# Order of work at a phase edge: spatial mixing put two steps earlier and kept in other tiles, half of a combination of h put into the next phase

## The chip, the cores and the metric

The kernel runs on one core of one Trainium2 chip. Its time is the device time of one execution in microseconds (us); several runs are given by their median and their extremes. Traces come from single profiled executions, and all stretches of time are counted from the start of such an execution's span.

## The reference

The reference computes one layer of a gated decoder with three parallel branches, for a prompt of 1024 tokens and for 8 x 8 sample tokens that share the weights (1088 tokens, width 1024). Cut to its core:

```python
h = rmsnorm(x, norm_g) * (1.0 + scale) + shift            # shift, scale, gate from silu(c) @ ada_w
z = h @ w_in + b_in                                       # one wide projection, columns split by use
vn = rmsnorm(a_v, gmlp_vnorm_g)                           # branch A: spatial gating
s = einsum('gts,bnsgc->bntgc', tril(gmlp_ws), vn) + gmlp_bs
ya = a_u * s * silu(a_g)
yb = sink_attention(...) * silu(b_g)                      # branch B: window of 128
yc = mlstm(...) * sigmoid(o) * silu(c_g)                  # branch C
gates = sigmoid(m_g)                                      # three gates per channel
merged = gates_a * (ya @ w_branch_a) + gates_b * (yb @ w_branch_b) + gates_c * (yc @ w_branch_c)
x_out = x + gate * (merged @ w_out)
```

## The kernel before

All operands are float32. A matrix is kept as two float32r parts, hi and lo (hi a rounded copy, lo what is left), and a product is three matmuls: hi·hi, hi·lo, lo·hi. So every operand must be split: a cast on ScalarE (ACT) writes hi, a subtraction on VectorE (DVE) writes lo. `hh[k]` and `hl[k]` are the two parts of h, 128 channels (k = 0 to 7) by 1088 tokens.

**Two phases meet here.** In the phase before the edge TensorE (PE) works on attention in 26 steps. In each step one pipeline stage of several blocks is issued (`q`, `s`, `p`, `v`, `y` of `Prompt` or `Sample`), and between them a filler of projection matmuls, the last of which make the gate of branch B (`bg_chunk`, tile `zb`). The order of PE's instructions is written out by hand in this phase (`manual_schedule`); in the others, and on the other engines, a scheduler orders instructions, and each engine takes its own in that order. The table `tail` gives what is added after certain steps. `Sample.v` ends in three small VectorE operations on the tile `ots`, and the transpose in `Sample.y` reads it.

**Spatial mixing.** `mix(g)` for the four channel groups is 18 matmuls (`pk<-WT,vn`, `pk<-WTs,vn`) into three PSUM banks and three VectorE evictions into the tile `sA[g]` (lines 1264 and 1269). Of the banks `pk` there are three in all, so a second mix waits for the evictions of the first. Before, the mixing of groups 0 and 1 follows steps 21 and 22, that of groups 2 and 3 follows step 25, the end of the phase.

**The last phase** forms a 2 x 2 block product in seven products instead of eight. For the weights of two column groups, and for h cut in two halves of its channels (k and k + 4) and of its tokens (b = 0, 1, each `HT` = 544), product q multiplies a combination of weights with a combination of h, `TT[q, k]`, k = 0 to 3. `TT[1]`, `TT[2]` and `TT[3]` are plain parts of h. `TT[5]` (`t_first`) and `TT[6]` (`t_second`) are made long before the edge. `TT[4]` (`t_third`: subtract twice, add, split into a tile `tc`) is made after steps 22, 23 and 25 in halves of 272. `TT[7]` (`t_in_place`) overwrites the second half of `hh[k]` and `hl[k]`, k = 0 to 3, which nothing reads afterwards in its old form; `x` and `y` in it are one tile. A product of one item is two halves of 272 tokens with 12 matmuls each, three for each k. `collect` gathers the results on VectorE.

**Weights of the last phase.** `seven(...)` makes the items of one pair of columns: a preparation (load `raw`, combine in `comb`, split into `prod` by `w_split`, lines 1365 and 1366) and a run. Preparations are issued five items ahead. There are five `raw` tiles and six `prod` tiles, so the split of a weight waits for the product six weights earlier. `items` lists the order in which products run. Group 0 of `it` runs its products in the order 1, 2, 5, 6, 3, 7, 4, the other groups in the order 1, 6, 7, 5, 3, 2, 4. Before, the list begins with all of `t_in_place`, then products 1, 2, 5, 6, 3 of group 0, product 1 of group 1, products 7 and 4 of group 0, and products 6 and 7 of group 1.

**Tiles.** `slot(tag, ...)` gives a named piece of SBUF that later tiles with this tag take over. A tile waits until the users of the one before it are done.

Of the kernel before, what the change touches and what calls it, by code (L numbers as in the profile page):

```python
# [37 lines left out]
def trunk_kernel(ctx: ExitStack, tc: tile.TileContext, I, O):  # L38
# [762 lines left out]
    drow = dp.tile([9, 1024], F32, name="drow")  # L801
    TT = {}
    sA = [None] * 4

# [14 lines left out]
    with tc.tile_pool(name="bph", bufs=1, side="right", reuse_waits="tile") as b1:  # L819
# [264 lines left out]
        class Sample:  # L1084
# [48 lines left out]
            def v(self):  # L1133
                g, bg = self.g, self.bg
                pO = pu_()
                mm(pO[:, 0:64], self.PT[:64, 128:256], vB[:64, 8, g], True, True)
                for b in range(4):
                    mm(pO[32 * b:32 * b + 32, 64:128], self.PT[:, 32 * b:32 * b + 32], vcn[0][:, 4 * bg + b, g], True, True)
                self.ot = bt([128, 64], "ots", bufs=2)
                V.tensor_copy(self.ot, pO[:, 0:64])  # L1140
                V.tensor_tensor(self.ot, self.ot, pO[:, 64:128], ALU.add)
                V.tensor_scalar(self.ot, self.ot, self.dn, 0.5, ALU.mult, ALU.mult)

# [55 lines left out]
        def t_tile(tag):  # L1199
            t = slot(tag, [128, 2, HT], F32R, name="tc")  # L1200
            return t[:, 0], t[:, 1]
# [25 lines left out]
        def t_third(k):  # L1227
            to = t_tile(("m4", "m5", "y6", "m0")[k])
            for j in range(2):
                t_next(gt(HC, "tx"), 4, k, k + 4, 0, 6, to, slice(HC * j, HC * j + HC))  # L1230
# [25 lines left out]
        def mix(g):  # L1256
            sA[g] = slot(("y2", "y3", "y7", "m1")[g], [128, NT], name="sA")
            bsb, WT = A["bsb"], A["WT"]
# [17 lines left out]
        def seq(*fs):  # L1276
            return lambda: [f() for f in fs]

        tail = {0: lambda: t_first(0), 1: lambda: t_first(1), 2: lambda: t_first(2), 3: lambda: t_first(3), 11: lambda: t_second(0), 13: lambda: t_second(1), 17: lambda: t_second(2),
                18: seq(lambda: t_second(3), a_scale), 20: a_load, 21: lambda: mix(0),  # L1280
                22: seq(lambda: mix(1), lambda: t_third(0)), 23: lambda: t_third(1),
                25: seq(lambda: mix(2), lambda: mix(3), lambda: t_third(2), lambda: t_third(3))}

# [79 lines left out]
    def w_split(x, tile=None):  # L1363
        t = tile if tile is not None else w2.tile([128, 2, 512], F32R, tag="prod", bufs=6, name="prod")
        S.copy(t[:, 0], x)  # L1365
        V.tensor_tensor(t[:, 1], x, t[:, 0].bitcast(F32), ALU.subtract)  # L1366
        return t

    def wk(t, part, k, n=128):
# [132 lines left out]
    def t_in_place(k):  # L1502
# [5 lines left out]
        TT[7, k] = t_split(x, half(hh, k, 1), half(hlo, k, 1))  # L1508

    def y_tiles(f):  # L1510
        yh[f] = y2[0].tile([128, NT], F32R, tag=f"yh{f}", name="yh")
        yl[f] = slot(("y2", "y3", "y7")[f - 1], [128, NT], F32R, name="yl") if f else y2[0].tile([128, NT], F32R, tag="yl0", name="yl")

# [38 lines left out]
    def y_load(n):  # L1552
        br = ORDER_BR[n]
        if not stage:
            stage.append(slot("m1", [128, 2, HT], name="stage"))
        for f in range(4):
# [88 lines left out]
    gr = [x for g in range(4) for x in gate_rows(g)]  # L1645
    items += [act(t_in_place, *((k,) for k in range(4)))] + it[0][:5] + it[1][:1] + it[0][5:]
    rest = it[1][1:3] + [None] + it[1][3:4] + [None] + it[1][4:5] + [None] + it[1][5:6] + [None] + it[1][6:] + [None]
    rest += it[2][:1] + [None] + it[2][1:2] + [None] + it[2][2:3] + [None] + it[2][3:] + it[3]
    items += [x or gr.pop(0) for x in rest]

    def gate_b(f, b):
        if not stage:
            stage.append(slot("m1", [128, 2, HT], name="stage"))
        x, y = stage[0][:, 0], stage[0][:, 1]
# [41 lines left out]
    KS8 = (0, 4, 1, 5, 2, 6, 3, 7)  # L1696
    SLOTS = (None, ("m4", "m5", "y6", "m0"), ("y0", "y1", "m2", "m3"), ("y4", "y5", "y2", "y3"))
    wo = {}
# [73 lines left out]
```

## Time and profile before

| what | us |
|---|---|
| median of 3 runs | 1217.87 |
| lowest, highest | 1213.67, 1218.21 |
| profiled execution, its time | 1217.25 |
| profiled execution, its span | 1215.5 |

The span is the stretch in which instructions run. A page gives the busy time of each engine, the span in 40 slices, the chain of waits and the costliest groups of instructions. In a group, `out<-in` are the program's names, L and a number is the line. PE is TensorE's matmuls, PEld its weight loads, DVE VectorE, ACT ScalarE, POOL GpSimd. A row of waits has the total, the count and the longest. A row of a table by windows has for each engine the busy time and the number of instructions that start there, then the clock that TensorE was granted (1.00 is full), the busy share of the DMA engines and GB/s.

| slices of 1/40 of the span (30.4 us) | 16 to 21 |
|---|---|
| from, to | 486 to 668 us |
| PE, tenths busy | 9 9 9 9 7 9 |
| DVE, tenths busy | 7 7 5 6 9 7 |

The edge between the two phases lies in the fifth of these.

### The profile page before, as it was taken

The page shows a single profiled execution, that of the slowest core. Times are in us where ns is not written, and L with a number is a line of the kernel's source. Part 1 is how long each engine was busy: PE and PEld are TensorE (multiplying, and loading weights), DVE is VectorE, ACT ScalarE, POOL GpSimd, SP SyncE. Part 2 cuts the span into 40 slices and gives each one's busy share as a digit, 9 for nine tenths or more (in the row PEclk, how much of TensorE's full clock was granted, in tenths as well). Part 3 has the DMA queues.
Part 4 walks back from the last instruction along what each step waited for, and adds up shares of the span by engine and source line. Part 5 has one row for each costly group of instructions (what it writes and reads, how often), then busy time and mean ns, then how long its engine had stood idle before and what let it go on. Part 6 is the DMA issues. An engine that isn't in the chain of part 4 may idle for free.

```text
span 1215.5 us, 23135 instructions
## 1 busy us (share of the span) xinstructions
PE 1166.3 (96%) x8900; PEld 1116.6 (92%) x8900; DVE 787.7 (65%) x1887; ACT 485.4 (40%) x1215; POOL 76.9 (6%) x111
## 2 busy tenths in 40 slices
PE   5899999999979999999979999999999999999998
PEld 2689999999969998888878999999999999999998
DVE  3477877755465677775697784655766676669333
ACT  3443454433432367896243432333333343236000
POOL 2100001011022110010100000000000000000000
PEclk8989999999989999999989999999999999999999
DMA  9731222233222210213233246523533354466332
GB/s 310 224 88 36 73 66 79 57 106 102 79 72 67 64 43 20 70 40 97 63 87 106 81 134 197 153 81 94 169 111 110 109 167 126 127 197 192 96 92 83
DMA packets 150773, 129.74 MB, mean 107 GB/s; under 512 B 13613, under 2 KB 140213, under 8 KB 150648
## 3 DMA queue, kind: packets, MB, share of 16 engines
q1 hardware_dynamic: 142984, 118.96, 33.4%
q0 software_dynamic: 2240, 7.08, 1.6%
q10 hardware_dynamic: 5440, 2.23, 0.7%
q8 instruction: 70, 1.15, 0.4%
q14 instruction: 39, 0.32, 0.1%
HBM read 99.39 MB, written 29.82 MB: 106 GB/s over the span
## 4 chain that ended last, share of the span: by engine, by line
PE 53%; DVE 3%; ACT 3%; DMA 1%; issue 1%; SPq 0%; ACTq 0%; DVEq 0%
PE pg L84 21%; PE pk L84 18%; PE pu L84 12%; ACT vn L1254 1%; DMA raw<-in_w_in_dram 0%; ACT Sm L1043 0%; DMA raw<-in_w_out_dram 0%; PE pu L88 0%; DVE prod L1366 0%; DVE sA L1264 0%; ACT hl L123 0%; ACT Sm L1051 0%; DVE ml L1573 0%; DVE tx L1219 0%; DVE wo L1366 0%
## 5 line engine op out<-in xcount | busy, mean ns | idle before, releaser
L84 PE MATMUL pg<-hl,hl 128*128 128x256 f32 (+3 forms) x904 | 279.1, 309 | 0.2 <-DVE hl L388 0.2
L84 PE MATMUL pg<-hh,hl 128*128 128x384 f32 (+1 forms) x912 | 240.9, 338 | 2.5 <-DVE hh L387 1.6
L84 PE MATMUL pg<-hl,hh 128*128 128x256 f32 (+1 forms) x1008 | 179.1, 285 | 0.2 <-ACT pg L1193 0.2
L84 PEld LDWEIGHTS pg<-hl,hl 128*128 128x128 f32 x904 | 172.3, 191 | 3.2 <-DVE hl L388 1.9
L84 PEld LDWEIGHTS pg<-hh,hl 128*128 128x128 f32 x912 | 163.8, 191 | 7.1 <-DVE hh L387 3.0
L84 PEld LDWEIGHTS pg<-hl,hh 128*128 128x128 f32 x1008 | 151.8, 190 | 0.7 <-ACT pg L1193 0.4
L1365 ACT CAST prod<-raw 128x512 fp32r<-128x512 f32 x76 | 47.2, 621 | 124.4 <-PE pk L84 62.0
L84 PE MATMUL pg<-hh,prod 128*128 128x272 f32 x400 | 84.7, 291 | 5.4 <-DVE prod L1366 3.0
L84 PE MATMUL pk<-hh,prod 128*128 128x272 f32 x368 | 78.6, 292 | 1.6 <-ACT hh L812 1.6
L84 PEld LDWEIGHTS pg<-hh,prod 128*128 128x128 f32 x400 | 66.7, 191 | 5.8 <-DVE prod L1366 3.2
L1366 DVE TENSOR_TENSOR prod<-raw,prod 128x512 fp32r<-128x512 f32 x76 | 52.1, 687 | 23.4 <-ACT prod L1365 23.3
L1365 ACT CAST prod<-comb 128x512 fp32r<-128x512 f32 x64 | 39.4, 616 | 65.4 <-PE pk L84 30.1
L1490 ACT ACTIVATE tt<-tt,bh 128x272 f32<-128x272 f32 x96 | 49.9, 523 | 38.9 <-DVE tt L1463 14.7
L84 PEld LDWEIGHTS pk<-hh,prod 128*128 128x128 f32 x368 | 61.7, 191 | 3.1 <-ACT hh L812 1.8
L84 PE MATMUL pk<-tc,prod 128*128 128x272 f32 x444 | 61.7, 288 | 0.0
L84 PE MATMUL pg<-yh,prod 128*128 128x272 f32 x288 | 60.1, 288 | 0.0
L84 PE MATMUL pk<-yh,prod 128*128 128x272 f32 x288 | 60.0, 288 | 0.0
L84 PEld LDWEIGHTS pk<-tc,prod 128*128 128x128 f32 x444 | 57.8, 188 | 0.9 <-DVE tt L1532 0.4
L84 PE MATMUL pg<-hl,prod 128*128 128x272 f32 x200 | 58.1, 290 | 0.0
L84 PE MATMUL pg<-tc,prod 128*128 128x272 f32 x408 | 57.5, 291 | 0.0
L84 PE MATMUL pk<-hl,prod 128*128 128x272 f32 x184 | 53.7, 292 | 1.0 <-DVE hl L813 1.0
L84 PEld LDWEIGHTS pg<-tc,prod 128*128 128x128 f32 x408 | 54.1, 191 | 0.4 <-issue 0.4
(512 smaller groups left out, 2630.0 us busy)
## 6 DMA issues: line engine op xcount, KB each, us to landing
raw<-in_w_in_dram SPq DMA_DIRECT2D x124, 256.0 KB
dmg<-tt SPq DMA_DIRECT2D x88, 136.0 KB
mprev<-dmg SPq DMA_DIRECT2D x64, 136.0 KB
adaraw<-in_ada_w_dram SPq DMA_DIRECT2D x16, 512.0 KB
stage<-dy SPq DMA_DIRECT2D x24, 272.0 KB
xt<-in_x_prompt_dram SPq DMA_DIRECT2D x8, 512.0 KB
graw<-in_ada_w_dram SPq DMA_DIRECT2D x16, 256.0 KB
raw<-in_w_out_dram SPq DMA_DIRECT2D x32, 128.0 KB
```

Source lines behind the costliest of these rows:

```text
L84: T.matmul(out, lhsT=lhsT, rhs=rhs, start=start, stop=stop)
L1254: S.activation(vn[g][:tn, n], vn[g][:tn, n], AF.Copy, scale=vq[:tn, n:n + 1])
L1365: S.copy(t[:, 0], x)
L1366: V.tensor_tensor(t[:, 1], x, t[:, 0].bitcast(F32), ALU.subtract)
L1490: S.activation(x, x, AF.Tanh, bias=bh[:, b:b + 1], scale=0.5)
```

## The change

The evictions of the mixing of groups 2 and 3 go to the tiles m4 and m5 instead of y7 and m1; those held vn of groups 0 and 1, the inputs of the mixing of groups 0 and 1. With that, group 2 is mixed after step 22 and group 3 after step 23. `t_third` of k = 0 and 1 follows steps 24 and 25 and writes y6 and m0. For k = 2 and 3 it is taken out of this phase: `t_late` makes `TT[4]` there in one piece of 544 instead of two of 272, in y7 and m1. The three operations on `ots` get a high priority with the scheduler.

In the last phase `t_in_place` no longer stands at the head of the list. It is issued in two parts, behind the split of the second and of the fourth weight; `t_late` follows behind that of the sixth. Products 7 and 4 of group 0 no longer follow one another: product 6 of group 1 comes between.

```diff
@@ tiles of TT[4]
+    T4S = ("y6", "m0", "y7", "m1")
@@ Sample.v
                 self.ot = bt([128, 64], "ots", bufs=2)
-                V.tensor_copy(self.ot, pO[:, 0:64])
-                V.tensor_tensor(self.ot, self.ot, pO[:, 64:128], ALU.add)
-                V.tensor_scalar(self.ot, self.ot, self.dn, 0.5, ALU.mult, ALU.mult)
+                with tc.high_priority():
+                    V.tensor_copy(self.ot, pO[:, 0:64])
+                    V.tensor_tensor(self.ot, self.ot, pO[:, 64:128], ALU.add)
+                    V.tensor_scalar(self.ot, self.ot, self.dn, 0.5, ALU.mult, ALU.mult)
@@ t_third, mix
-            to = t_tile(("m4", "m5", "y6", "m0")[k])
+            to = t_tile(T4S[k])
...
-            sA[g] = slot(("y2", "y3", "y7", "m1")[g], [128, NT], name="sA")
+            sA[g] = slot(("y2", "y3", "m4", "m5")[g], [128, NT], name="sA")
@@ tail
-                22: seq(lambda: mix(1), lambda: t_third(0)), 23: lambda: t_third(1),
-                25: seq(lambda: mix(2), lambda: mix(3), lambda: t_third(2), lambda: t_third(3))}
+                22: seq(lambda: mix(1), lambda: mix(2)), 23: lambda: mix(3), 24: lambda: t_third(0), 25: lambda: t_third(1)}
@@ w_split and what is issued behind a split
-        S.copy(t[:, 0], x)
-        V.tensor_tensor(t[:, 1], x, t[:, 0].bitcast(F32), ALU.subtract)
+        a = S.copy(t[:, 0], x)
+        b = V.tensor_tensor(t[:, 1], x, t[:, 0].bitcast(F32), ALU.subtract)
+        splits.append((a.ins, b.ins))
         return t
+
+    splits = []
+
+    def behind(f, n, *ks):
+        def run(_):
+            with tc.issue_after(splits[n][0]), tc.issue_after(splits[n][1]):
+                for k in ks:
+                    f(k)
+
+        return (None, run)
@@ the last phase
+    def t_late(k):
+        x = y2[0].tile([128, 2, HT], F32, tag="yh1", name="tx")[:, 0]
+        t_next(x, 4, k, k + 4, 0, 6, t_tile(T4S[k]), slice(0, HT))
...
-        yl[f] = slot(("y2", "y3", "y7")[f - 1], [128, NT], F32R, name="yl") if f else y2[0].tile([128, NT], F32R, tag="yl0", name="yl")
+        yl[f] = slot(("y2", "y3", "m4")[f - 1], [128, NT], F32R, name="yl") if f else y2[0].tile([128, NT], F32R, tag="yl0", name="yl")
...
-            stage.append(slot("m1", [128, 2, HT], name="stage"))
+            stage.append(slot("m5", [128, 2, HT], name="stage"))
...
-    items += [act(t_in_place, *((k,) for k in range(4)))] + it[0][:5] + it[1][:1] + it[0][5:]
-    rest = it[1][1:3] + [None] + it[1][3:4] + [None] + it[1][4:5] + [None] + it[1][5:6] + [None] + it[1][6:] + [None]
+    items += it[0][:2] + [behind(t_in_place, 1, 0, 1)] + it[0][2:4] + [behind(t_in_place, 3, 2, 3)] + it[0][4:5] + it[1][:1]
+    items += [behind(t_late, 5, 2, 3)] + it[0][5:6] + it[1][1:2] + it[0][6:]
+    rest = it[1][2:3] + [None] + it[1][3:4] + [None] + it[1][4:5] + [None] + it[1][5:6] + [None] + it[1][6:] + [None]
...
-    SLOTS = (None, ("m4", "m5", "y6", "m0"), ("y0", "y1", "m2", "m3"), ("y4", "y5", "y2", "y3"))
+    SLOTS = (None, ("y7", "m1", "y6", "m0"), ("y0", "y1", "m2", "m3"), ("y4", "y5", "y2", "y3"))
```

Three places in the order of the engines. TensorE, the end of the attention phase: `pk<-WT,vn` and `pk<-WTs,vn` are a mix, `pu<-ident,ots` the transpose in `Sample.y`, `pg<-hh,hl` and `pg<-hl,hl` the filler, and `pg<-hh_250,prod` the first matmul of the last phase (a number behind hh or hl tells the tiles apart).

```order
 L84 MATMUL pg<-hl_569,hl 128x320
 L84 MATMUL pg<-hh_568,hl 128x320
+L84 MATMUL pk<-WT,vn 128x128 x8
+L84 MATMUL pk<-WTs,vn 128x64
 L88 MATMUL pu<-ident,ots 64x128
 L84 MATMUL pu<-vB,PTs 128x64
 L84 MATMUL pu<-vcn,PTs 32x64 x4
 L88 MATMUL pu<-ident,ots 64x128
-L84 MATMUL pk<-WT,vn 128x128 x8
-L84 MATMUL pk<-WTs,vn 128x64
-L84 MATMUL pk<-WT,vn 128x128 x8
-L84 MATMUL pk<-WTs,vn 128x64
```

Behind the last transpose of an attention output there were two mixes; now there is none, and one of them has moved ahead of these transposes (the other lies further ahead).

VectorE, the head of the last phase. `tx` is the scratch tile of the combinations of h, `tc` the lo part of `TT[4]`, `sA` an eviction of the mixing, `prod<-raw` the lo part of a weight, `hl_251<-tx` the lo part of `TT[7]`. Before:

```order
L1264 SCALAR_TENSOR_TENSOR sA<-pk,cols,bsb 128x512
L1269 SCALAR_TENSOR_TENSOR sA<-pk,cols,bsb 128x64
L813 TENSOR_TENSOR tc<-tx,tc 128x272 x3
L1505 TENSOR_TENSOR tx<-hh_387,hh_250 128x544
L1506 TENSOR_TENSOR tx<-hl_388,hl_251 128x544
L1507 TENSOR_TENSOR tx<-tx 128x544
L1366 TENSOR_TENSOR prod<-raw_7086,prod 128x512
L813 TENSOR_TENSOR hl_251<-tx,hh_250 128x544
L1366 TENSOR_TENSOR prod<-raw_7088,prod 128x512
```

The change:

```order
L1266 SCALAR_TENSOR_TENSOR sA<-pk,cols,bsb 128x512
L1271 SCALAR_TENSOR_TENSOR sA<-pk,cols,bsb 128x64
L1219 TENSOR_TENSOR tx<-hh_387,tc 128x272 x2
L1142 COPY ots<-pu 128x64
L1220 TENSOR_TENSOR tx<-tx,tc 128x272 x2
L1143 TENSOR_TENSOR ots<-ots,pu 128x64
L1221 TENSOR_TENSOR tx<-tx,hl_388 128x272 x2
L1144 TENSOR_SCALAR ots<-ots,dns 128x64
L814 TENSOR_TENSOR tc<-tx,tc 128x272
```

The last eviction of the mixing used to stand directly ahead of the last splits of `TT[4]`; now all of `t_third` for k = 0 and 1 stands behind it. The first weight follows at the end of that block:

```order
L1221 TENSOR_TENSOR tx<-tx,hl_404 128x272 x2
L814 TENSOR_TENSOR tc<-tx,tc 128x272 x2
L1367 TENSOR_TENSOR prod<-raw_7060,prod 128x512
L1367 TENSOR_TENSOR prod<-raw_7062,prod 128x512
L1517 TENSOR_TENSOR tx<-hh_387,hh_250 128x544
L1518 TENSOR_TENSOR tx<-hl_388,hl_251 128x544
```

The first two weights are split ahead of the first in-place combination, which used to stand ahead of them.

VectorE, behind the last part of `TT[7]`, where the results of product 7 of group 0 are used (`tt`, `tg` and `yl` are results, gate and output of group 0). Before:

```order
L1544 SCALAR_TENSOR_TENSOR tt<-tg,tt 128x272
L1480 TENSOR_TENSOR tt<-pk,tt 128x272
L1543 SCALAR_TENSOR_TENSOR tt<-tt,cols 128x272
L1366 TENSOR_TENSOR prod<-raw_7145,prod 128x512
L1360 TENSOR_TENSOR comb<-raw_7629,raw_7631 128x512
L1548 TENSOR_TENSOR yl<-tt,yh 128x272
```

The change:

```order
L1220 TENSOR_TENSOR tx<-tx,tc 128x544
L1559 SCALAR_TENSOR_TENSOR tt<-tt,cols 128x272
L1367 TENSOR_TENSOR prod<-raw_7157,prod 128x512
L1221 TENSOR_TENSOR tx<-tx,hl_569 128x544
L1564 TENSOR_TENSOR yl<-tt,yh 128x272
L1361 TENSOR_TENSOR comb<-raw_7617,raw_7619 128x512
L1462 TENSOR_TENSOR tt<-pk,tt 128x272
L1560 SCALAR_TENSOR_TENSOR tt<-tg,tt 128x272
L814 TENSOR_TENSOR tc<-tx,tc 128x544
```

`t_late` for k = 3 stands between the work on the results, and its last row is what product 4 of group 0 reads.

More of the change, by code (lines that the diff above doesn't have):

```diff
@@ L1652, in gate_b @@
         if not stage:
-            stage.append(slot("m1", [128, 2, HT], name="stage"))
+            stage.append(slot("m5", [128, 2, HT], name="stage"))
         x, y = stage[0][:, 0], stage[0][:, 1]
```

## The prediction

> **What bounds the kernel now.** First the page: how much of the span TensorE works.
>
> ```profile
> span 1215.5 us, 23135 instructions
> ...
> PE 1166.3 (96%) x8900; PEld 1116.6 (92%) x8900; DVE 787.7 (65%) x1887; ACT 485.4 (40%) x1215; POOL 76.9 (6%) x111
> ```
>
> TensorE (PE) is busy 96% of the span, so a change that leaves the matmuls as they are, as this one does, can only move the gaps in between. The windows table shows where they are around the edge between the two phases.
>
> ```profile
> 600.00:612.00 12.00, 7.04 (x48) 6.26 (x47) 11.36 (x31) 4.13 (x13) 0.54 (x1) 0.86 0.08 20
> 612.00:620.00 8.00, 4.97 (x23) 4.84 (x22) 7.86 (x14) 3.09 (x6) 0.00 (x0) 0.58 0.00 0
> 620.00:640.00 20.00, 17.41 (x137) 16.99 (x136) 19.45 (x37) 8.42 (x16) 0.00 (x0) 1.00 0.47 132
> ...
> 660.00:700.00 40.00, 40.00 (x329) 36.19 (x329) 32.06 (x76) 16.35 (x35) 0.00 (x0) 1.00 0.30 88
> ...
> 800.00:900.00 100.00, 100.00 (x800) 100.00 (x799) 60.58 (x123) 34.82 (x66) 0.00 (x0) 1.00 0.40 115
> ```
>
> The columns are length, PE, PEld, DVE (VectorE), ACT, POOL, granted clock, DMA share, GB/s. From 600 to 640 PE misses 5.0 + 3.0 + 2.6 = 10.6 us, and VectorE is the engine that is full: 38.7 of 40. Later PE is full, so what is late there is late at the end, one for one. The waits of PE name the gaps:
>
> ```profile
> PE pg L84 <- DVE prod L1366: 3.0, 1, 3.0
> PE pu L88 <- DVE ots L1142: 2.5, 1, 2.5
> PE pg L84 <- ACT prod L1365: 2.4, 1, 2.4
> ...
> PE pk L84 <- ACT hh L812: 1.6, 1, 1.6
> PE pk L84 <- DVE hl L813: 1.0, 1, 1.0
> ```
>
> 5.4 us wait for the first split weight (prod), 2.5 for the last sample's attention output (ots), 2.6 for the in-place combination that product 7 reads (hh, hl). All three hang on one queue. VectorE alone, in two windows:
>
> ```profile
> 589.90:604.60 14.70, 11.16 (x35) 0.95 0.21 63
> 604.70:639.40 34.70, 34.47 (x67) 0.88 0.27 76
> ```
>
> From 604.7 until the last hl is split VectorE works 34.47 of 34.70 us. So the question is not which wait is removed, but **where the work of VectorE goes, and which product of TensorE stands behind it**.
>
> **The change, part by part.** Durations on VectorE:
>
> ```profile
> 604.08 0.43 DVE L1218 TENSOR_TENSOR tx<-tx,tc 128x272 f32<-128x272 f32 x1
> ...
> 605.46 0.78 DVE L1217 TENSOR_TENSOR tx<-hh,tc 128x272 f32<-128x272 f32 x2
> ...
> 638.73 0.72 DVE L813 TENSOR_TENSOR hl<-tx,hh 128x544 fp32r<-128x544 f32 x1
> ```
>
> ```profile
> L1264 DVE SCALAR_TENSOR_TENSOR sA<-pk,cols,bsb 128x512 f32<-128x512 f32 x4 | 3.0, 746 | 0.3 <-PE pk L84 0.3
> ...
> L1519 DVE SCALAR_TENSOR_TENSOR tt<-tt,cols,sA 128x272 f32<-128x272 f32 x4 | 1.9, 494 | 0.0
> ...
> L1269 DVE SCALAR_TENSOR_TENSOR sA<-pk,cols,bsb 128x64 f32<-128x64 f32 x2 | 0.5, 274 | 0.0
> ```
>
> The first fence is the timeline (start, length, operation, count), the second the groups by shape (busy us, mean ns). Two 272-wide operations take 0.78 us with 0.43 each, so the next starts after 0.35. By the same overlap of 0.08 a 544-wide one (0.72) occupies 0.64.
>
> *Half of t_third moved.* For k = 2, 3 it has 2 x 2 x 4 = 16 operations 272 wide, 16 x 0.35 = 5.6 us, that leave the stretch before the last hl. They come back as t_late: 2 x 4 operations 544 wide, 8 x 0.64 = 5.1 us, right behind that hl and, by the order of VectorE, before anything that product 4 of group 0 needs.
>
> *Mixing sooner.* Matmuls and evictions stay the same in number. But t_third of k = 0, 1 now stands behind mix(3), and so behind TensorE:
>
> ```profile
> 599.42 0.27 PE L88 MATMUL pu<-ident,ots 128*64 128x128 f32 x1
> ...
> 606.78 2.05 PE L84 MATMUL pk<-WT,vn 128*128 128x128 f32 x16
> 608.76 0.43 PE L84 MATMUL pk<-WTs,vn 64*128 64x64 f32 x2
> ```
>
> A mix takes 2.2 us at full clock. TensorE did not stall before 600.3, so the work ahead of 599.42 plus mix(2) ends at 601.6, and the first group of mix(3) at about 602.6; VectorE can take it at 602.8. Before, it used the idle time of the first window for all of t_third(0) and most of t_third(1). Now it idles there, and this is what the earlier mixing costs.
>
> What VectorE must do from 602.8 to the last hl is the 34.47 us of the old stretch, less the 13 moved operations that lay in it (4.6; the third of the 16 starts at 604.08), less mix(2)'s evictions (0.75 + 0.75 + 0.27 in duration, 1.5 occupied), plus one zb and the three ots steps (0.8), plus all 16 operations of t_third(0) and (1) (5.6): **34.8 us**. To this come waits for ACT inside the queue.
>
> ```profile
> L812 ACT CAST hh<-tx 128x544 fp32r<-128x544 f32 x4 | 2.6, 648 | 4.9 <-DVE tx L1507 4.9
> L812 ACT CAST tc<-tx 128x272 fp32r<-128x272 f32 x6 | 2.3, 417 | 7.2 <-DVE tx L1219 7.2
> ```
>
> In the new order the last hl stands directly behind the tx that ACT must cast first, so 0.65 plus hand-over, 0.8; the first splits wait 0.4 for casts of tc and prod; two dependent pairs add 0.2. With 1.4 the last hl is ready at 602.8 + 34.8 + 1.4 = **639.0**. Before it was 639.45. The 5.6 us taken out bring product 7 only 0.45 us, since the start of the queue slid.
>
> *Item order.* Product 7 of group 0 is followed by product 6 of group 1 and then product 4, which reads t_late. From the last hl to the last tc split VectorE has t_late's 5.1 us and 14 other operations: three 512 wide (0.68 as in rival C's rows, 0.6 occupied), seven TENSOR_TENSOR 272 wide (0.35) and four SCALAR_TENSOR_TENSOR (0.49 less the overlap, 0.41): 1.8 + 2.5 + 1.6 = 5.9. Sum 11.0, and 0.6 of waits for the cast of tc and dependent steps: the last tc at **650.6**.
>
> TensorE meanwhile:
>
> ```profile
> 615.16 0.82 PE L84 MATMUL pg<-hh,prod 128*128 128x272 f32 x2 [3.03 <-DVE prod L1366]
> ...
> 644.41 1.67 PE L84 MATMUL pk<-tc,prod 128*128 128x272 f32 x12
> 645.92 1.66 PE L84 MATMUL pg<-tc,prod 128*128 128x272 f32 x12
> 647.42 1.66 PE L84 MATMUL pk<-tc,prod 128*128 128x272 f32 x12
> 648.91 0.29 PE L84 MATMUL pu<-hh,prod 128*128 128x272 f32 x1
> ```
>
> Half a product (12 matmuls) takes 1.5 us. The first weight is split when VectorE has done 8.0 us of its list (mix(3)'s evictions, zb, ots and t_third) and the 0.4 of waits, at 602.8 + 8.4 = 611.2, so the products start at about 611.5; before, they got going at 615.16. Until product 7 needs its last hl there are six products (18 us, and some 2 for the clock) and nine matmuls, so PE waits from about 632.6 to 639. Then the rest of 7 (1.8, more at half clock), product 6 of group 1 (3.0) and nine matmuls of product 4 (1.1): 645 to 646.5. Then **a new wait until 650.6**, where the old kernel had none. Behind it 14 matmuls of product 4 remain, 1.8 us at full clock and 3.5 at half.
>
> Which clock the trace shows behind gaps of this kind:
>
> ```profile
> 600.30:602.80 2.50, 0.00 (x0) 0.00 (x0) 2.43 (x9) 1.14 (x5) 0.54 (x1) 1.00 0.08 13
> 603.00:606.00 3.00, 3.00 (x16) 3.00 (x16) 2.72 (x8) 0.41 (x2) 0.00 (x0) 0.51 0.25 71
> ...
> 636.50:639.50 3.00, 0.42 (x2) 0.19 (x1) 2.95 (x6) 1.23 (x2) 0.00 (x0) 1.00 0.00 0
> 641.00:644.00 3.00, 3.00 (x15) 3.00 (x14) 2.36 (x6) 1.98 (x4) 0.00 (x0) 0.50 0.00 0
> ```
>
> Both gaps, 2.5 us and 2.6 of 3.0, are followed by three microseconds at half clock, the second only from about 640.6 on, one microsecond after work resumed. So I take half of the 14 matmuls at half clock, 2.6 us, and keep 1.8 and 3.5 as ends.
>
> The Trainium skill, "TensorE: Matmul & The Clock Gate", section "HAM oscillation — how this bites in real kernels", gives as the abstract rule that gaps longer than about 3.4 us are to be avoided. The trace differs: 2.5 us were enough for a clock of 0.51. By that rule alone the new gap of four or more microseconds would put all 14 matmuls at half clock, 0.9 us more than I take; by the rows a shorter gap would not save them either.
>
> **The sum.** Nine products are done at 650.6 + 0.1 + 2.6 = 653.3, against 648.91 before: **+4.4 us**. From there TensorE was full, so the end moves as much: 1217.25 us of the profiled execution (span 1215.5) become 1221.65. The median of the runs shown is 1217.87, 0.6 above that execution; I predict **1222**. The forecast's own bounds: with none of the 2.0 us of waits in the VectorE queue and full clock, 648.6 + 0.1 + 1.8 = 650.5, +1.6; with all 14 matmuls at half clock, 654.2, +5.3. With that 0.6, this is 1219.5 to 1223.2, and a run scatters by some two microseconds around (1213.67 to 1218.21 before).
>
> What costs nothing: the stage in m5 for m1, yl in m4 for y7 and the w_out slots trade tiles whose old users are the same or long done, and the high priority for ots does not show in VectorE's order ahead of the mixing. The first gap of PE does shrink: products start at about 611.5 instead of 615.16, but that lead is waited off at product 7.
>
> **The rivals.**
>
> *A, it does what one would hope: the moved work falls into free time of VectorE.* Then only the front gap is left; PE starts at 611.5, runs nine products in 27 us and loses some 2 us to the clock: 640.5, 8.4 us sooner, **1209**. It decides if the last hl is there by about 633 and the last tc by 637. For it speaks the lower VectorE load from 660 on (32 of 40). Against it: t_late stands in the queue ahead of what is free, and 34.47 of 34.70 leave no room. Chance 0.07.
>
> *B, no difference: VectorE starts on h sooner than I say.* If t_third did not stand behind the wait for mix(3), it would have some 3.5 us of idle time in the first window (14.70 less 11.16). The last tc comes at 647.2, the nine products end at 649.1 at full clock: +0.2, **1218**. For it: that idle time is real. Against it: VectorE takes its instructions in the order given, and that order has the evictions of mix(3) first. It is the case in which the earlier mixing does not hold VectorE up at all. Chance 0.13.
>
> *C, clearly slower: a transfer becomes the wait.* One raw buffer of the next group is freed only by the lo split of the weight of product 2 of group 1 (row prod<-raw_7153), and the comb that reads what is loaded into it (row comb<-raw_7617,raw_7619) stands three rows ahead of the last tc. In the old trace:
>
> ```profile
> 643.30 0.69 DVE L1366 TENSOR_TENSOR prod<-raw,prod 128x512 fp32r<-128x512 f32 x1
> ...
> 647.49 0.68 DVE L1360 TENSOR_TENSOR comb<-raw,raw 128x512 f32<-128x512 f32 x1
> ```
>
> ```profile
> 645.00:646.00 1.00, 1.00 (x10) 1.00 (x9) 0.90 (x3) 0.53 (x1) 0.00 (x0) 1.00 0.72 176
> 646.00:647.00 1.00, 1.00 (x10) 1.00 (x9) 0.88 (x3) 0.83 (x2) 0.00 (x0) 1.00 0.29 86
> ```
>
> Split done at 644.0, 262 KB moved by 647.0, so 3.0 us; the comb came 0.5 us later and did not wait. In the new order nine operations (3.7 us) lie between. Two microseconds more for the transfer would bring the last tc to about 651.9, and the longer gap the full half clock: 655.5, +6.6, **1224** and above. Chance 0.20.
>
> **How the numbers follow.** The forecast has 0.60, C 0.20, B 0.13, A 0.07. About 0.5% (6.1 us) is what a measurement of this kernel can tell from no change. Faster by more is A alone: 0.07. Slower by more is C and a tenth of the forecast: 0.26. Within it lie the rest of the forecast and B: 0.67. The range takes in the forecast's bounds with the scatter, B, and most of C: 1216 to 1226. It leaves out A and the far end of C.
>
> **What would show it.** Right: the wait for prod of some 3 us and that for ots merge into one idle stretch of TensorE from about 604.5 to 611.5; VectorE idles while PE mixes, then is full from 602.8 to 650; PE waits six microseconds for hh and hl ahead of product 7, and anew, some four, for a tc of L814 ahead of the last quarter of the first half of product 4. Each step has its own sign of error: an hl earlier than 637 would say that the VectorE queue was summed wrongly; no wait for tc would say that t_late is hidden (A); a wait of VectorE for raw would be C. The prediction is wrong as a whole if TensorE's idle time between 600 and 655 is below its old 10.6 us; I expect some 15.

## The result, and the profile after

| what | before | changed |
|---|---|---|
| runs shown, us | 1217.87, 1218.21, 1213.67, 1213.74 | 1224.55, 1221.43, 1221.65, 1224.28 |
| median, us | 1215.8 | 1222.97 |
| span of the profiled execution, us | 1215.5 | 1222.8 |

The ratio is 1.0063 (95% interval 1.0045 to 1.008): the change makes the kernel slower by 0.6%. Nine more runs of the changed kernel, in a later comparison, had a median of 1220.46 and a ratio of 1.0048 (1.003 to 1.0066), there against a median of 1215.46. The forecast was 1222, from a median before of 1217.87.

The waits of TensorE in the changed kernel, from 520 to 760 us (total, count, longest):

```profile
PE pk L84 <- ACT hh L813: 3.7, 2, 3.2
PE pg L84 <- ACT prod L1366: 3.4, 1, 3.4
PE pu L88 <- DVE ots L1144: 2.6, 1, 2.6
...
PE pg L84 <- ACT tc L813: 1.7, 1, 1.7
PE pg L84 <- DVE tc L814: 1.2, 1, 1.2
PE pk L84 <- DVE hl L814: 1.1, 2, 0.9
```

Against the list of before, three things differ. The wait for prod is 3.4 us and no longer 5.4. The wait for hh and hl, ahead of and in product 7, has grown from 2.6 to 4.8. And 2.9 us of waiting for tc are new. The sum is 13.7 us, before it was 10.6: **3.1 us more**.

The windows of the same trace (length, PE, PEld, DVE, ACT, POOL, granted clock, DMA share, GB/s):

```profile
600.00:612.00 12.00, 6.25 (x51) 5.44 (x49) 8.75 (x26) 3.65 (x11) 0.54 (x1) 0.81 0.10 23
612.00:620.00 8.00, 7.76 (x41) 7.54 (x42) 7.92 (x14) 4.59 (x10) 0.00 (x0) 0.65 0.11 27
620.00:640.00 20.00, 15.33 (x115) 14.36 (x113) 19.14 (x36) 6.33 (x13) 0.00 (x0) 0.95 0.43 121
640.00:660.00 20.00, 16.95 (x108) 15.79 (x109) 18.17 (x38) 7.48 (x15) 0.00 (x0) 0.79 0.21 54
```

VectorE, which worked 11.36 of the first 12 us before, now works 8.75; then it is full to 640, and nearly so behind. TensorE is full from 612 to 620 (before, 4.97 of 8), at a clock of 0.65, and misses 4.7 us behind and then 3.1, where it missed 2.6 and, from 640 to 660, nothing. What VectorE waits for in that first stretch, from 590 to 612, before and then in the changed kernel:

```profile
DVE zb L1167 <- ACT zb L1166: 2.0, 1, 2.0
...
DVE sA L1264 <- PE pk L84: 0.3, 1, 0.3
```

```profile
DVE zb L1169 <- ACT zb L1168: 4.4, 2, 3.4
DVE sA L1266 <- PE pk L84: 2.2, 2, 1.7
```

With `t_third` behind the mixing, VectorE stands still while TensorE works: 6.6 us in these two rows, where it was 2.3.

Two executions do not reach the edge at the same moment. The row of VectorE that can serve as a clock is the last but one zb, the end of the projections; of before, and of the changed kernel:

```profile
593.78 0.56 DVE L1167 SCALAR_TENSOR_TENSOR zb<-tb,zb 128x384 f32<-128x384 f32 x1 [2.03 <-ACT zb L1166]
```

```profile
594.72 0.56 DVE L1169 SCALAR_TENSOR_TENSOR zb<-tb,zb 128x384 f32<-128x384 f32 x1 [3.43 <-ACT zb L1168]
...
639.38 0.73 DVE L814 TENSOR_TENSOR hl<-tx,hh 128x544 fp32r<-128x544 f32 x1 [0.71 <-ACT hh L813]
...
650.95 0.72 DVE L814 TENSOR_TENSOR tc<-tx,tc 128x544 fp32r<-128x544 f32 x1
```

The profiled execution of the changed kernel is 0.94 us late here, and was already at a zb row 17 us sooner (577.06 and 578.00). TensorE from its start on the products to the end of the first nine:

```profile
612.24 0.59 PE L84 MATMUL pg<-hh,prod 128*128 128x272 f32 x1 [3.36 <-ACT prod L1366]
...
639.39 0.60 PE L84 MATMUL pk<-hh,prod 128*128 128x272 f32 x1 [3.20 <-ACT hh L813]
...
647.15 1.29 PE L84 MATMUL pg<-tc,prod 128*128 128x272 f32 x9
650.11 0.39 PE L84 MATMUL pg<-tc,prod 128*128 128x272 f32 x1 [1.68 <-ACT tc L813]
...
651.72 0.82 PE L84 MATMUL pg<-tc,prod 128*128 128x272 f32 x2 [1.22 <-DVE tc L814]
652.34 2.92 PE L84 MATMUL pk<-tc,prod 128*128 128x272 f32 x12
...
655.06 0.33 PE L84 MATMUL pu<-hh,prod 128*128 128x272 f32 x1
```

The tenth product starts at 655.06; before, at 648.91. From the zb row it is 60.34 us, before 55.13. **This stretch, from the last but one zb to the tenth product, is the measure used below.** It is 5.2 us longer. The windows table of just this stretch, before and then in the changed kernel, says in what:

```profile
593.78:648.91 55.13, 44.55 (x310) 42.44 (x310) 51.49 (x113) 21.06 (x46) 1.09 (x2) 0.88 0.23 62
```

```profile
594.72:655.06 60.34, 46.63 (x310) 43.55 (x310) 54.09 (x111) 19.71 (x43) 1.09 (x2) 0.83 0.23 64
```

The same 310 matmuls keep TensorE busy for 2.1 us more, at a granted clock of 0.83 in place of 0.88, and the other 3.1 us are idle time. The rest of the 7.3 us by which the two spans differ: 0.94 ahead of the edge, 0.55 less between the tenth product and the wait for mh at the end of the kernel (mh and ml are the two parts of the merged rows that the last matrix product reads), and 1.7 more behind that wait. The last term shows in the clock; the first 10 us from the start of that wait, of before, and of the changed kernel:

```profile
1113.65:1123.65 10.00, 8.00 (x65) 7.80 (x66) 8.38 (x20) 4.11 (x10) 0.00 (x0) 1.00 0.47 148
```

```profile
1119.25:1129.25 10.00, 7.99 (x53) 7.78 (x53) 7.67 (x18) 4.05 (x10) 0.00 (x0) 0.83 0.47 135
```

Both kernels wait 2.0 us for mh and ml there; only in the changed one a stretch at half clock follows.

### The profile page after: what moved, and what is told of

Same layout as the page of the kernel before. It is cut to its first block, busy times and chain, and to the rows that moved or that the text cites. A ratio compares the mean times of both kernels' runs of the same rounds, so it can differ in the third digit from the quotient of the medians.

```text
span 1222.8 us, 23120 instructions
## 1 busy us (share of the span) xinstructions
PE 1171.5 (96%) x8900; PEld 1120.7 (92%) x8900; DVE 787.9 (64%) x1879; ACT 484.8 (40%) x1213; POOL 76.9 (6%) x111
## 4 chain that ended last, share of the span: by engine, by line
PE 45%; DVE 3%; DMA 1%; issue 1%; ACT 0%; SPq 0%; DVEq 0%; ACTq 0%
PE pk L84 17%; PE pg L84 17%; PE pu L84 11%; DMA mgr<-dmg 0%; DMA raw<-in_w_out_dram 0%; DVE prod L1367 0%; DVE ml L1589 0%; DVE wo L1367 0%; DVE tt L1614 0%; ACT mh L1588 0%; DVE tt L1616 0%; DVE hl L814 0%; DVE tc L814 0%; DVE tx L1519 0%; DVE tx L1219 0%
```

## The experiments

In each the stretch is taken from its own profile, the ratio is to the kernel before on the same chip. A stretch is one profile: those of the two runs of the changed kernel differ by 0.4 us, and those of the two tries without `t_late`, whose waits agree to 0.8 us, by 1.8. So a difference of one or two microseconds between two stretches decides nothing by itself.

| run | stretch, us | against before | median, us | ratio (95% interval) |
|---|---|---|---|---|
| before | 55.13 | | 1215.2 to 1215.8 | |
| changed | 60.34 | +5.2 | 1222.97 | 1.0063 (1.0045 to 1.008) |
| changed, again | 60.72 | +5.6 | 1220.46 | 1.0048 (1.003 to 1.0066) |
| t_late left out, first try | 56.08 | +1.0 | 1220.81 | 1.0055 (1.0039 to 1.0072) |
| t_late left out, second try | 54.30 | -0.8 | 1215.36 | 0.9994 (0.998 to 1.0007) |
| early mixing, nothing moved | 60.76 | +5.6 | 1220.66 | 1.0043 (1.0024 to 1.0062) |
| old mixing, half moved | 58.64 | +3.5 | 1219.73 | 1.0037 (1.0021 to 1.0053) |
| old mixing, only in-place and items | 55.98 | +0.9 | 1216.08 | 1.0009 (0.9993 to 1.0026) |
| old order of items | 62.57 | +7.4 | 1221.48 | 1.0058 (1.0035 to 1.008) |
| t_late on GpSimd | 62.87 | +7.7 | 1223.02 | 1.0074 (1.0049 to 1.0099) |
| before, in-place sums on TensorE | 49.84 | -5.3 | 1210.58 | 0.995 (0.9935 to 0.9964) |
| changed, all sums on TensorE | 51.31 | -3.8 | 1214.48 | 0.9984 (0.9973 to 0.9995) |
| changed, in-place sums on TensorE | 49.33 | -5.8 | 1212.82 | 0.9986 (0.9971 to 1.0) |

**The theory:** VectorE's queue is full across the edge, and each half of the change lengthens what stands ahead of something that TensorE needs. **The rivals:** only one half does harm, or the loss arises elsewhere.

### What t_late costs

```diff
-    items += [behind(t_late, 5, 2, 3)] + it[0][5:6] + it[1][1:2] + it[0][6:]
+    TT[4, 2], TT[4, 3] = TT[6, 2], TT[6, 3]
+    items += it[0][5:6] + it[1][1:2] + it[0][6:]
```

> The changed kernel without t_late: product 4 of group 0 reads the tiles of product 6 for k = 2, 3, so eight 544-wide operations of VectorE (and two casts of ACT) are left out. Queue theory: nothing ahead of the last hl changes (ready at 639 to 640), TensorE still waits some 5 to 6 us ahead of and in product 7, but the two waits for tc (1.7 + 1.2 us) are gone, and behind product 7 the remaining 15 matmuls of product 4 follow at once: ninth product done at about 649.2 instead of 655.1, kernel 1216 to 1219. Rival 1 (the earlier mixing alone costs the time, t_late was hidden): no change, 1221 to 1224. Rival 2 (the rest of the loss is a clock phase at the end of the kernel, not these waits): less than 3 us gained.

Measured: the waits for tc are gone and the stretch falls to 56.08 us, but the median is 1220.81. What was won at the edge was given back at the end. Its waits of TensorE from 760 on:

```profile
PE pk L84 <- ACT mh L1588: 4.6, 1, 4.6
PE pk L84 <- DVE ml L1589: 1.6, 1, 1.6
```

One cast ahead of it waited for a transfer that came late (mgr, the merged rows read back), in the timeline of ACT:

```profile
1102.69 1.10 ACT L1588 CAST mh<-mgr 128x1088 fp32r<-128x1088 f32 x1 [0.81 <-DMA mgr<-dmg]
```

That could be a bound at the end which swallows every gain, or an artefact of the edit: product 4 of the last group now read the tiles m2 and m3, into which mgr is loaded. So the edit was made otherwise:

```diff
+    TT[4, 2], TT[4, 3] = TT[4, 0], TT[4, 1]
```

> The changed kernel without t_late again, but product 4 of group 0 (and of the later groups) now reads the tiles of k = 0, 1 in place of k = 2, 3, so that no tile of product 6 is held longer; what is left out is the same: eight 544-wide operations of VectorE, two casts. In the first version the matmuls ended 8.5 us sooner than in the changed kernel, but TensorE then waited 6.2 us instead of 2.0 for mh, behind two transfers of mgr into m2, m3, which product 4 of the last group still read. Theory (that wait was made by the longer use of m2, m3): it shrinks to about 2 us, the stretch from the last but one zb to the tenth product stays at 56.1 us (60.3 in the changed kernel, 55.1 before), and the kernel takes 1214 to 1218. Rival (the end of the kernel is bound by VectorE and the transfers, whatever the edge does): the wait for mh stays at 5 us or more, 1219 to 1222.

Measured: the stretch is 54.30, one wait of 1.2 us for ml is left, the median is 1215.36. So the first try had lengthened the use of m2 and m3, and the end of the kernel is no bound of its own. Without `t_late`, eight operations of VectorE and two casts of ACT, the stretch is 4.3 to 6.4 us shorter, by the two tries and the two profiles of the changed kernel, and in the second try the kernel is level with the kernel before. The two tries differ in the clock: from 638.9 to 641.0 us, behind the same wait of 3.2 us at nearly the same time, it was 0.50 in the first and 1.00 in the second.

### Each half by itself

The early mixing, with all of `t_third` behind it and nothing moved:

```diff
-                22: seq(lambda: mix(1), lambda: mix(2)), 23: lambda: mix(3), 24: lambda: t_third(0), 25: lambda: t_third(1)}
+                22: seq(lambda: mix(1), lambda: mix(2)), 23: lambda: mix(3), 24: lambda: t_third(0),
+                25: seq(lambda: t_third(1), lambda: t_third(2), lambda: t_third(3))}
-    items += [behind(t_late, 5, 2, 3)] + it[0][5:6] + it[1][1:2] + it[0][6:]
+    items += it[0][5:6] + it[1][1:2] + it[0][6:]
```

> The changed kernel with all of t_third back in the old phase, behind mix(3); no t_late; same computation. Queue theory: the 16 operations 272 wide (5.6 us) stand ahead of the first split weight again, so the products start at about 617.5 (612.2 in the changed kernel), the last hl is ready at about 645 (640.1), no wait for tc; ninth product done at 653 to 655; kernel 1221 to 1224, so the earlier mixing by itself costs about what the whole change costs. Rival 1 (t_late alone is to blame): last hl at 639.5, time of the kernel before, 1214 to 1218. Rival 2 (the queue takes t_third into idle time of the mixing): last hl at 641 to 642, 1217 to 1220.

```profile
PE pg L84 <- ACT prod L1367: 9.5, 1, 9.5
PE pk L84 <- ACT hh L813: 3.8, 2, 3.2
...
PE pk L84 <- DVE hl L814: 1.5, 2, 1.3
```

Measured, counted from the zb row: the products start at 23.6 us (changed kernel 17.5), the last hl is done at 51.3 (45.4). Eight operations for each of two k stand ahead of the first weight and cost 6 us there; the wait for prod is 9.5. The stretch is 60.76: as slow as the whole change, without any t_late. (This run and the next have the new place of the in-place combination and the new order of items too; what those cost is measured behind them.)

The old mixing, with the half moved:

```diff
-                22: seq(lambda: mix(1), lambda: mix(2)), 23: lambda: mix(3), 24: lambda: t_third(0), 25: lambda: t_third(1)}
+                22: seq(lambda: mix(1), lambda: t_third(0)), 23: lambda: t_third(1),
+                25: seq(lambda: mix(2), lambda: mix(3))}
```

(sA, T4S, yl, stage and SLOTS take the tiles of the kernel before, T4S its m4, m5, y6, m0.)

> The old mixing (order and tiles of the kernel before) with t_third of k = 2, 3 moved into the last phase as in the change; same computation. Queue theory: 13 operations of the full stretch (4.6 us) leave, so the last hl is ready at 634.5 to 636 (639.45 before), TensorE waits some 2 us less ahead of product 7, and waits anew for tc, whose last split is ready 11.6 us behind the last hl, at 646 to 647.5; ninth product done at 648.5 to 650.5 (648.9 before); kernel within 2 us of the kernel before, 1214 to 1218. Rival 1 (t_late alone makes the loss, wherever the mixing stands): 1221 to 1224. Rival 2 (moved work is hidden): ninth product at 645 or sooner, 1211 to 1213.

Measured: 1219.73, and the stretch is 3.5 us longer; I had expected none. From its last hl to its last tc it is 11.6 us, as expected. But the last hl is done at 43.7 us behind the zb row and not at 41: of the 4.6 us taken out ahead of it only 2 arrive. The waits of VectorE from 590 to 612, and those of TensorE, say where the others are:

```profile
DVE sA L1266 <- PE pk L84: 2.8, 3, 1.0
```

```profile
PE pk L84 <- ACT hh L813: 5.7, 2, 3.2
...
PE pg L84 <- ACT tc L813: 1.9, 1, 1.9
PE pg L84 <- DVE tc L814: 1.5, 1, 1.5
```

Without t_third behind it the queue of VectorE runs dry and waits 2.8 us for the matmuls of the mixing (0.3 before). Work that covered a wait was taken away.

What remains in the last phase, the place of the in-place combination and the order of items, alone on the kernel before (with `behind` and the rest of `items` as in the change):

```diff
-    items += [act(t_in_place, *((k,) for k in range(4)))] + it[0][:5] + it[1][:1] + it[0][5:]
+    items += it[0][:2] + [behind(t_in_place, 1, 0, 1)] + it[0][2:4] + [behind(t_in_place, 3, 2, 3)] + it[0][4:5] + it[1][:1]
+    items += it[0][5:6] + it[1][1:2] + it[0][6:]
...
```

> The kernel before with nothing but the new place of the in-place combination (behind the splits of weights 1 and 3 instead of ahead of them) and the new order of items (product 6 of group 1 ahead of product 4). In the three runs that have these, VectorE took 26.4 to 26.6 us from the first lo split of a weight to the last hl; before it took 24.3. Theory 1 (the new place draws collections and splits ahead of the last hl and costs some 2 us by itself, which the moved half has to win back first): stretch from the last but one zb to the tenth product 57 to 58 us (55.1 before), kernel +2 to +3. Theory 2 (the place only swaps work of VectorE around, and all work ahead of the last hl is the same): 55 to 56 us, kernel within 1 us of before.

Measured: 55.98 us and a ratio whose interval holds 1. At the edge it costs 0.9 us, less than two profiles can differ by. So the loss is in the two halves, 5.6 and 3.5 us alone (each with this remainder in it), and they do not add up: together they cost 5.2 to 5.6. The reason would be that the moved work shortens the very queue that the early mixing delays. The high priority for `ots` was not run by itself; TensorE's wait for ots is 2.5 us before and 2.6 in the changed kernel.

The order of items alone, product 4 directly behind product 7 in the changed kernel:

```diff
-    items += [behind(t_late, 5, 2, 3)] + it[0][5:6] + it[1][1:2] + it[0][6:]
+    items += [behind(t_late, 5, 2, 3)] + it[0][5:] + it[1][1:2]
```

> The changed kernel with product 4 of group 0 directly behind product 7 again, product 6 of group 1 behind it. If product 6 covers the wait for tc: TensorE reaches the last quarter of the first half of product 4 three microseconds sooner and waits that much longer, while four collections fewer stand in VectorE's queue ahead of the last tc (some 1.5 us); product 6 then follows behind. Stretch to the tenth product 61 to 63 us (60.3), kernel 0.5 to 3 us slower than the changed kernel, 1222 to 1226. Rival (the order is worth nothing): 60.3 within 1 us.

```profile
PE pg L84 <- ACT tc L813: 4.0, 1, 4.0
...
PE pg L84 <- DVE tc L814: 0.3, 1, 0.3
```

Measured: 62.57 us, some 2 us more than the changed kernel; 4.3 us of waits for tc in place of 2.9. The product in between does cover part of t_late: 1.4 us by the waits. In the whole time, 1221.48 beside 1220.46 in the same comparison, the intervals overlap.

The changed kernel again, for the scatter:

> The changed kernel again, no edit, for the scatter of its steps: the stretch from the last but one zb to the tenth product (60.3 us in its profile) should repeat within 1.5 us, the time between the tenth product and the wait for mh (464.2) within 0.5, what lies behind (103.6) within 2. Ratio to the kernel before 1.004 to 1.008.

Measured: 60.72, 464.51 and 104.3 us, ratio 1.0048. The steps repeat, each wait at the edge to 0.1 us. Most of what scatters lies ahead of them: the zb row starts at 589.83 us here, at 594.72 in the first profile.

### Is it the queue? Two ways to empty it

GpSimd (POOL) is idle behind the edge, so t_late was given to it:

```diff
+    def t_sum(k):
...
+        G.tensor_tensor(x, h32(hh, k + 4, 0), TT[6, k][0].bitcast(F32), ALU.subtract)
+        G.tensor_tensor(x, x, TT[6, k][1].bitcast(F32), ALU.subtract)
+        G.tensor_tensor(x, x, h32(hlo, k + 4, 0), ALU.add)
...
+        S.copy(hi, x)
+        G.tensor_tensor(lo, x, hi.bitcast(F32), ALU.subtract)
+    items += [act(t_sum, (2,), (3,))]
```

> The changed kernel with t_late on GpSimd, which is idle there: three sums for each of k = 2, 3 first thing in the last phase, the lo split later; the casts stay on ACT; same computation. Estimate from the 128x1024 TENSOR_TENSOR of POOL in the trace (2380 ns): 1.3 us for one 544 wide, six sums in 8 us, done by about 615, the last tc by about 630. Queue theory: as with t_late left out: the waits for tc are gone, ninth product at about 649, 1216 to 1219. Rival 1 (the work of POOL slows VectorE, whose operations get longer while POOL runs): last hl 2 us or more later than 640, 1219 to 1223. Rival 2 (POOL needs over three times as long for an operation): the wait for tc stays, 1221 or more.

It gained nothing: the highest median and the longest stretch of the table, if by little. Its wait of TensorE for the attention output:

```profile
PE pu L88 <- DVE ots L1144: 8.0, 1, 8.0
```

The groups of POOL from 600 to 618 (busy us, mean ns of one), then those of VectorE in the same window, first with POOL at work, then in the changed kernel:

```profile
L1528 POOL TENSOR_TENSOR tx<-hh,tc 128x544 f32<-128x544 f32 x2 | 3.1, 1589 | 0.1
L1529 POOL TENSOR_TENSOR tx<-tx,tc 128x544 f32<-128x544 f32 x2 | 3.0, 1524 | 0.0
L1530 POOL TENSOR_TENSOR tx<-tx,hl 128x544 f32<-128x544 f32 x2 | 2.8, 1430 | 0.0
```

```profile
L1220 DVE TENSOR_TENSOR tx<-tx,tc 128x272 f32<-128x272 f32 x4 | 3.7, 963 | 0.0
...
L1143 DVE TENSOR_TENSOR ots<-ots,pu 128x64 f32<-128x64 f32 x1 | 0.2, 208 | 0.0
```

```profile
L1220 DVE TENSOR_TENSOR tx<-tx,tc 128x272 f32<-128x272 f32 x4 | 1.6, 434 | 0.0
...
L1143 DVE TENSOR_TENSOR ots<-ots,pu 128x64 f32<-128x64 f32 x1 | 0.2, 215 | 0.0
```

The mean of VectorE's four operations in the first row is 963 ns in place of 434. Two of them lie beside POOL's work and take 2.92 us together, the two behind it 0.78 as in the changed kernel. While POOL works its 9 us, VectorE hardly gets on; the operation with one input in PSUM keeps its 0.2 us, but the next one, which completes ots for TensorE, does not:

```profile
610.73 1.32 DVE L1144 TENSOR_SCALAR ots<-ots,dns 128x64 f32<-128x64 f32 x1
```

In the changed kernel it takes 0.25 us. The last hl is done at 53.3 us behind the zb row, 7.9 later. My estimate for POOL (1.3 us for an operation, 1.4 to 1.6 measured) was near; that VectorE would be free meanwhile was wrong, and the first rival came true.

TensorE idles in the same stretch. Four matmuls by plus and minus the identity, which accumulate in a bank of PSUM, make a sum of four tiles; ACT casts, VectorE only splits:

```diff
...
+            for i, t in enumerate(plus + minus):
+                mm(ps, pm1[0][:, i // 2], t[:, c], i == 0, i == 3)
+            S.copy(to[0][:, c], ps)
+            V.tensor_tensor(to[1][:, c], ps, to[0][:, c].bitcast(F32), ALU.subtract)
...
+        pe_sum((half(hh, k + 4, 1), half(hlo, k + 4, 1)), TT[7, k], TT[7, k])
```

On the kernel before, for the in-place combination alone:

> The kernel before, but the three sums of the in-place combination for each k (twelve operations 544 wide, 7.7 us of VectorE) are made by TensorE: four matmuls 272 wide by plus and minus the identity into a bank for each half, 32 in all, estimated 4 us at 0.125 us each; ACT casts and VectorE subtracts from the bank (8 operations 272 wide in place of 4 544 wide). Queue theory (VectorE's queue sets the last hl, and TensorE idles meanwhile): last hl some 7 us sooner, TensorE's idle time there falls from 10.6 to about 3 to 5 us while it works 4 us more; stretch to the tenth product 51 to 54 us (55.1), kernel 1 to 4 us faster. Rival (the matmuls of the sums stand ahead of the products and the banks come free only as VectorE gets to them): no gain, 55 to 57 us.

```profile
PE pu L88 <- DVE ots L1142: 2.5, 1, 2.5
PE pg L84 <- ACT pm L1507: 1.8, 1, 1.8
```

(pm is the tile with plus and minus the identity.)

Measured: no wait for prod, hh or hl is left, the idle time is 4.3 us, the stretch 49.84, better than the 51 to 54 expected. The last hl is done at 24.9 us behind the zb row (45.7 before). The kernel takes **1210.58 us, 0.5% less than before (ratio 0.995, 0.9935 to 0.9964)**: it beats both.

All sums on TensorE, on the changed kernel:

> The changed kernel with all sums of the in-place combination and of product 4 (t_third and t_late, k = 0 to 3) on TensorE by plus and minus the identity: 64 matmuls 272 wide, estimated 8 us at 0.125 us; ACT casts, VectorE has only the lo splits, 16 operations 272 wide. Queue theory: VectorE has some 15 us less ahead of the last hl and tc, products start at 14 us behind the last but one zb, no wait for hh, hl or tc remains; stretch to the tenth product 13 + 27 + 8 + 1.5 for the clock = 49.5 us, 48 to 52 (60.3 in the changed kernel, 55.1 before), kernel 1208 to 1213. Rival 1 (the waits for ots and prod stay, and 8 us of matmuls are added to a full TensorE): 55 us or more, no gain over the kernel before. Rival 2 (banks of PSUM are held by the sums until VectorE and ACT evict them, which stalls the products): waits for pg, pk, pu by 5 us or more.

Measured: 51.31 us, 1214.48. No wait for hh, hl or tc, and none of 5 us for a bank; but 3.0 us of waits for ots, the identity and the first weights stayed, the products start 17.7 us behind the zb row and not 14, and the forecast stretch was 1.8 us too short. TensorE works 48.29 of the 51.31 us. The next run (49.33) leaves product 4 to VectorE and has 32 matmuls, 4 us, less: moving those too won nothing here and seems to lose 2.0 us, which two single profiles don't prove. Once VectorE has room, TensorE is the full engine.

Last, the change on top of the in-place sums:

> The change on top of the kernel whose in-place sums TensorE makes: early mixing and t_late for k = 2, 3 as in the changed kernel, the in-place sums by 32 matmuls with plus and minus the identity, all four k first thing in the last phase. Queue theory (the change costs only because VectorE's queue is full until product 4): with 7 us less in that queue t_late stands among the products and is hidden, no wait for hh, hl or tc remains; the products start 21 to 23 us behind the last but one zb, the stretch to the tenth product is 49 to 51 us, as with the in-place sums on TensorE alone (49.8), and the kernel takes 1209 to 1212. Rival (the early mixing or the moved half cost by themselves, each 3 to 5 us as in the runs with one of them): stretch 53 us or more, 1214 or more.

Measured: stretch 49.33, like the 49.84 without the change. t_late stands among the products, and no wait for hh, hl or tc is left. **At the edge the change costs nothing once the queue has room**, which is what the theory says and the rival denies. The median is 1212.82 nevertheless, 2.2 above the kernel with the sums alone and just above the 1209 to 1212 that I expected, and the intervals of the two ratios do not meet. In the profiles 1.1 us more lie between the tenth product and the wait for mh, where a wait of 1.6 for gsb (a row of the gate) at 666 us is new, and 1.2 more behind it. So on top of the sums the change is still no gain; why it costs time behind the edge was not looked into.

## Why the prediction was right

Its numbers against the trace, with 0.94 us taken off for the late start of the profiled execution:

| step | predicted | measured |
|---|---|---|
| VectorE takes the first group of mix(3) | 602.8 | 602.9 |
| products start | 611.5 | 611.3 |
| last hl ready | 639.0 | 639.2 |
| last tc ready | 650.6 | 650.7 |
| 14 matmuls behind it | 2.6 us | 3.3 us |
| nine products done | 653.3 | 654.1 |
| idle time of TensorE | some 15 us | 13.7 us |
| wait for hh and hl at product 7 | some 6 us | 4.8 us |
| new wait at product 4 | some 4 us | 2.9 us |

The mechanism was the one forecast. That the time came within 1 us of 1222 is in part luck: the forecast was 4.1 us above a median of 1217.87 of three runs, and with the fourth run that median fell to 1215.8. The change itself is 7.2 us by the medians of the first comparison and 5.0 by those of the second, both more than forecast.

**The queue.** The sum of VectorE's queue held to 0.2 us. The 5.6 us taken out ahead of the last hl bring almost nothing, since the early mixing lets the queue start later; the run with the early mixing and nothing moved shows that start as a loss of its own, its last hl 5.6 us later than before. The 11.6 us from hl to tc held too, here and in the run with the old mixing. That t_late is on the path is shown by leaving it out, though the size of its share scatters from 4.3 to 6.4 us.

**The clock** was the term mis-sized. I took half of the 14 matmuls at half clock; from 651.72 to 655.06 all are, 3.3 us in place of 2.6, and this is nearly all of the 0.8 us that the forecast of +4.4 lacks to +5.2. And product 7 and its follower ran slower than I had it, so TensorE came to product 4 at 648.4 (647.5 with the start taken off) and not at 645 to 646.5: part of what I called a wait was slow work. The opening sentence, that a change with the same matmuls can only move the gaps, was too narrow for the same reason: 2.1 of the 5.2 us are matmuls that run slower.

**The end.** "From there TensorE was full, so the end moves as much" left out 1.7 us behind the wait for mh (1.7 and 2.5 in the two profiles of the changed kernel). With 0.94 ahead of the edge, 5.2 at the edge and less 0.55 before the end, this makes the 7.3 us between the two profiled executions. It need not belong to the change: with the early mixing and nothing moved, and with the old order of items, the time behind that wait was only 0.3 and 0.5 us longer than before. What lets the clock fall behind a gap of two microseconds there in some profiles and not in others was not settled.

**The rivals.** A needed the last hl by 633 and fell with the waits for tc. B needed VectorE to start on h during the mixing; its queue took the evictions first, as said. C needed a wait for raw: among VectorE's waits from 612 to 660 there is none.

**What the prediction had not seen:** that t_third of k = 2 and 3, too, covered a wait of VectorE in the old order; that of k = 0 and 1 it had. It did not bear on the sum, since the changed kernel mixes early; it made my expectation for the half moved alone some 3 us too good.

## What to carry to other kernels

Where one engine's queue is full across a phase edge, moving work along that queue only moves the wait to its next reader; ask which other engine idles in the same stretch and whether it can do the work. Before an operation is moved away, look whether it covers a wait of its own engine, and before it is given to a free engine, whether the two share a path. Compare executions from a common row just ahead of the edge, not from the start of the span: here that row alone lay between 589.8 and 594.7 us.

## What the runs showed of the hardware

**Half the clock can follow a wait of 1.8 us.** TensorE's timeline of the kernel before with the in-place sums on TensorE:

```profile
609.83 0.59 PE L84 MATMUL pg<-hh,pm 128*128 128x272 f32 x1 [1.76 <-ACT pm L1507]
...
612.72 0.43 PE L84 MATMUL pg<-hh,pm 128*128 128x272 f32 x1
612.95 0.43 PE L84 MATMUL pg<-hl,pm 128*128 128x272 f32 x1
613.17 0.34 PE L84 MATMUL pg<-hh,pm 128*128 128x272 f32 x1
613.35 0.29 PE L84 MATMUL pg<-hl,pm 128*128 128x272 f32 x1
613.47 0.29 PE L84 MATMUL pk<-hh,pm 128*128 128x272 f32 x1
```

Behind the wait a matmul follows the one before it after 0.23 us, from 613.3 on after 0.125: 3.4 us at half clock. In the changed kernel the waits of 1.7 and 1.2 us, with one matmul between them, were followed by 3.3 us of it. The Trainium skill, "TensorE: Matmul & The Clock Gate", section "HAM oscillation — how this bites in real kernels", warns of gaps over some 3.4 us; by these rows gaps half as long can be followed by half clock too. They need not be: behind the 1.3 and 0.7 us at the end of the kernel before it stayed at 1.00. Nor is the length of the slow part fixed, as the two tries without `t_late` show.

**GpSimd held VectorE up** where both read SBUF: 2.92 us in place of 0.78 for the same two operations. The Trainium skill, "SBUF — State Buffer", section "SBUF: two separate sides", has the rule: the two share a port pair that is locked for a whole instruction, against a VectorE operation with two SBUF inputs. The trace agrees, also in what goes free, the operation with an input in PSUM (208 ns beside 215). The operation with one tensor input in SBUF (L1144) was held as well, 1.32 us in place of 0.25; why was not looked into. My expectation for that run had the slowdown only as a rival.
